# Two thirds of each feed-forward's way down as seven half-size products, behind the column tiles of the way up

## The chip, the cores and the metric

The kernel runs on one core of a Trainium2 chip. The metric is the device time of one execution in microseconds. Times before are from three runs; one further execution was profiled, and all views of the trace are of that one.

## The reference

A decoder trunk of two layers on 512 tokens of width 1024, all in float32. Layer 0 mixes tokens by dilated attention, layer 1 by a recurrent block (RG-LRU); each is followed by a feed-forward, and each of the four parts sits between two RMS norms:

```python
def conv_ffn(x, w_up, conv_w, conv_b, w_down):
    u = causal_dwconv(x @ w_up, conv_w, conv_b)
    g, v = u[..., :D_FF], u[..., D_FF:]
    return (jax.nn.gelu(g, approximate=True) * v) @ w_down

for layer in range(DEPTH):
    h = rms_norm(x, norm_mix_pre[layer])
    h = attention or rglru (h)
    x = x + rms_norm(h, norm_mix_post[layer])
    h = rms_norm(x, norm_ffn_pre[layer])
    h = conv_ffn(h, ffn_w_up[layer], ...)      # 1024 -> 2 x 3072 -> 1024
    x = x + rms_norm(h, norm_ffn_post[layer])
```

The change is in the two feed-forwards alone.

## The kernel before

**A matrix product.** Every float32 operand is split in two float32r parts, `hi` (a copy by ScalarE) and `lo` (the remainder, by VectorE), and three matmuls stand for one: hi x hi, hi x lo, lo x hi (`PASSES`, `mm3`). A weight goes from DRAM into a `raw` tile of 1 MB (two buffers), from there in two pieces ("units" of 128 x 1024) into `whi` and `wlo` (`pump`, `low_parts`), of which eight are held. The list `plan`, written at the end of the program, sets which weights are loaded and in which order they are split; `splits` keeps that order. `tick` is called after each piece of TensorE work: it lets waiting side work go on and splits one or two more units. Every engine takes its instructions in the order in which the program issues them.

**The way up.** The 6144 columns of `w_up` are cut in column tiles of 128 features by 512 tokens (`feat`: 8 x 3 matmuls of 512 columns, bank `ps`). A step of `j` has two gate tiles and two value tiles; each gets a convolution over tokens (one ScalarE step, two VectorE steps), the gate tile a gelu, the value tile a multiply with its gate tile. The results are `gv[0]` to `gv[23]`, 24 tiles of 128 x 512 that are the operand of the way down.

**Sevenths.** `PAIRS` lists which two steps go together. In a pair marked True the gate columns of both steps, a product of 512 tokens x 1024 x 512 columns, are computed by seven half-size products instead of eight (Strassen's scheme as arranged by Winograd), each 24 matmuls of 256 columns into a bank `vq`. The token sums `T` that they need are made once a layer. Sums of weights are not computed by an engine: they come up in the tile `sum`, into which POOL's queue adds one corner after the other with accumulating DMAs (`add_up`; kinds `first`, `sum`, `mix`), each allowed once the units of the one before have been split (`after`, `finished`).

**The way down.** `rows_proj` and `rows_run` multiply `gv` with the 3072 rows of `w_down`, 12 chunks of 256 rows: for each of four token tiles two banks `acc` of 512 columns, 24 x 3 matmuls each. When a token tile is complete, `norms` runs as side work: `postnorm` (L511 to L518), `prenorm`, and the transposes `tr` into the `hT` of the next layer. The last feed-forward has no `prenorm`, and its `postnorm` sends out the result.

In attention the values of two head groups are also made by seven products, of 512 columns each (`product`, L965); that function is moved by the change, so that the feed-forward can call it too.

**Memory.** `x` slots: eight tiles of 128 x 1024 that hold the residual, token sums or raw weights in turn. `gen` tiles: 29 of 128 x 512, for `gv` and all else. The `sum` tile and the norms' gains share one buffer.

Of the kernel before, what the change touches and what calls it, by code (L numbers as in the profile page):

```python
# [11 lines left out]
F32 = mybir.dt.float32  # L12
# [80 lines left out]
def kernel(  # L93
# [82 lines left out]
    raws, units, late = {}, {}, []  # L176
    sides, first_tiles = [], []

    total = {"open": True, "tile": None, "next": 0}
    finished, after, todo = set(), {}, {}  # L180

    def add(kind, kd, cols, srcs, behind=None, own=True):
# [99 lines left out]
    def add_up(i):  # L282

        kind, kd, cols, srcs = plan[i]
        if total["tile"] is None:
            total["tile"] = cp.tile([P, 512 // cols, 4, cols], F32, tag="gain", name=nm("sum"))
        tile_, at = total["tile"], 0
        part = tile_[:, int(kind[-1] == "1")]
        for src, m in srcs:
            dst = part[:, :, at : at + m]  # L290
            if kind[:5] == "first":
                nc.sync.dma_start(dst, src)
            else:
                nc.gpsimd.dma_start(dst, src, accum_op=ALU.add)
            at += m
        raws[i] = tile_ if kind == "mix" else part
        total["next"] += 1
# [219 lines left out]
            if final:  # L517
                nc.sync.dma_start(out[0, t * P : (t + 1) * P, i * 512 : (i + 1) * 512], xh[i])  # L518

    def norms(t, banks, post_g, pre_g, hT, spill):  # L520
        state["hold"] = t >= 2
        postnorm(t, banks, post_g, hT is None)
        if spill:
            nc.sync.dma_start(spill[t], xs_sb[t])
        if hT is not None:
            yield from prenorm(t, hT, pre_g, 3 if t == 3 else 4)
        if t == 3:
            state["hold"] = False
            total["open"] = True
# [14 lines left out]
    def token_sums(hT):  # L544
# [37 lines left out]

        return (lambda name: lambda a: made[name][a]), make

    def feat_tiles(n, hT, sink, halves=False, between=None, at=None):

        if halves:
            ids = [chunk() for _ in range(n)]
            W = {}
            banks = [psum() for _ in range(2 * n)]  # L590
            for hf in range(2):
                for j in range(2 * n):
                    if not hf:
                        W[j] = take(ids[j // 2], j % 2)
                    feat(W[j], hT, banks[j], hf * 256, hf * 256 + 256)
                    if hf:
                        done()
                        sink(j, banks[j])
                    tick()
            return  # L600
        for c in range(n):
            i = chunk() if at is None else at
            for m in range(2):
                ps = psum()
                feat(take(i, m), hT, ps, 0, S)
                done()
                sink(2 * c + m, ps)
                tick()
                if between:
                    between()  # L610

    def rows_proj(nchunks, act, order, post, pre, spill=None):
# [12 lines left out]
        def run():  # L625
            return rows_run(nchunks, A, prep, seq, order, post, pre, spill)

        return prep, run

    def rows_run(nchunks, A, prep, seq, order, post, pre, spill):  # L630
        total.update(open=False, tile=None)
        post_g, pre_g = gains(*[g for g in (post, pre) if g is not None])
        hT = new_hT() if pre is not None else None
        W, banks = {}, {}
        left = {}
# [3 lines left out]
        for tiles, chunks in order:  # L639
            for c in chunks:  # L640
                if c not in W:
                    i = chunk()
                    W[c] = (i, 0), (i, 1)
                last = len(tiles) == 1
                if last:
                    prep(seq.index(2 * c) + 4)
                    loop = [[(tiles[0], i, kk) for i in range(2) for kk in range(2)]]
                else:
                    loop = [[(t, i, kk) for t in tiles for i in range(2)] for kk in range(2)]
                for n, part in enumerate(loop):  # L650
                    prep(seq.index(2 * c + n) + 3)
                    for t, i, kk in part:
                        k = 2 * c + kk
                        if t not in banks:
                            banks[t] = [psum("acc"), psum("acc")]
                            left[t] = [2 * nchunks, 2 * nchunks]
                        mm3(
                            banks[t][i],
                            [a[:, t * P : (t + 1) * P] for a in A[k]],
                            [v[:, 0, i * 512 : (i + 1) * 512] for v in take(*W[c][kk])],  # L660
                            left[t][i] == 2 * nchunks,
                            left[t][i] == 1,
                        )
                        left[t][i] -= 1
                        uses[k] -= 1
                        if not uses[k]:
                            done()
                    for t in tiles:
                        if left[t] == [0, 0]:
                            side(norms(t, banks[t], post_g, pre_g, hT, spill))  # L670
                    tick()
        state["rows"] = False
        return hT
# [69 lines left out]
    def ffn(layer, hT, post, pre, spill):  # L743
# [15 lines left out]
        def gated(b, ps, k):  # L759
# [5 lines left out]
            else:  # L765
                gv[k] = u

        total_of, make = token_sums(hT)

        def sevenths(j, n):  # L770
# [55 lines left out]

            side(ends())

        order = [([0, 1, 2, 3], range(9)), ([0], range(9, 12)), ([1], range(9, 12))]
        order += [([2, 3], [9]), ([2], [10, 11]), ([3], [10, 11])]  # L830
        prep, run = rows_proj(12, act_split(gv), order, post, pre)
        for js, wide in PAIRS:
            n = state["next"]
            steps = sevenths(js[0], n) if wide else None
            at = iter(WIDE_STEPS if wide else (0,) * 16)

            def between():
                for _ in range(next(at)):
                    next(steps, None)
                    tick()  # L840

            for j in js:
                if j == 11:
# [7 lines left out]
                feat_tiles(1 if wide else 2, hT, sink, j == 0, between, (n + 3 + 3 * (j - js[0])) if wide else None)  # L851
            if wide:
                state["next"] += 9
        for t in range(4):
            xs_sb[t] = load_x(t, src=spill[t])
        return run()

    def attention(hT, post, pre, spill):
# [96 lines left out]
                    vs.append(o)  # L955
                tick()

        def product(banks, act):
            i = chunk()
            for j in range(2):  # L960
                W = take(i, j)
                for u in range(2):
                    for k in range(2):
                        for n, (a, b) in enumerate(PASSES):
                            mm(  # L965
                                banks[u],
                                act(a)[:, 2 * j + k, u * P : (u + 1) * P],
                                W[b][:, k, :],
                                start=(j, k, n) == (0, 0, 0),
                                stop=(j, k, n) == (1, 1, 2),  # L970
                            )
                done()

        def value_steps(p0):

            vds = [dp.tile([S, 512], F32, name=f"vrows{p0 + i}") for i in range(2)]
            vrows.update({p0: vds[0], p0 + 1: vds[1]})
            def two():
                return [psum("vq") for _ in range(2)]
# [6 lines left out]
            def each(dst, a, b, op):  # L986
                for u in range(2):
                    nc.vector.tensor_tensor(dst[u], a[u], b[u], op=op)

            def steps():  # L990
                q = two()
# [7 lines left out]
                each(o, c, q, ALU.add)  # L999
                out(0, 0, o)  # L1000
                yield
                chunk()
                q = two()
                y = [gen(s="y") for _ in range(2)]
                product(q, total_of(3))
# [14 lines left out]
                each(o, y, q, ALU.subtract)  # L1020
                out(1, 0, o)
                yield
                chunk()
                q = two()
                product(q, total_of(1))
                each(y, y, q, ALU.add)
# [379 lines left out]
    def value_part(*at):  # L1406
        if at in VALUE_STEPS:
            for q in next(parts):
                n = w_quarter(*q, behind=chain[-1])
                if q[0] == "sum":  # L1410
                    chain.append((n, 1))

    for hp in range(4):
        if hp % 2 == 0:
            w_value(qkv, (2 * D + hp * 256, 512))
# [9 lines left out]
    for layer in range(2):  # L1425
        if layer:
# [6 lines left out]
            for c in range(4):  # L1433
                w_rows(lru_w_out[0], c * 256, "pair")
        w_up, ends = ffn_w_up[layer], {}
        for js, wide in PAIRS:
            if not wide:
                for j in js:
                    w_cols(w_up, j * 256)
                    w_cols(w_up, D_FF + j * 256)  # L1440
# [80 lines left out]
```

## Time and profile before

| | |
|---|---|
| median of 3 runs | 1470.57 us (1470.45 to 1471.04) |
| profiled execution | 1470.15 us, of which the span is 1468.4 |
| granted TensorE clock | 0.996 of full speed |
| TensorE busy | 1455.4 us, 99% of the span |
| VectorE, ScalarE, GpSimd busy | 64%, 45%, 5% |
| feed-forward of layer 0 | way up 523.4 to 781.5 us, way down to 913.8 us |
| feed-forward of layer 1 | way up 1072.8 to 1330.9 us, way down to 1461.5 us |
| after the last matmul | 6.9 us |

The stages are read from the chain that ended last, which runs through TensorE nearly everywhere. "PE" is TensorE's matmuls, "PEld" its weight loads, "DVE" VectorE, "ACT" ScalarE, "POOL" GpSimd, which here only issues DMAs, "SP" the queue that issues the other DMAs. A row of the trace's groups reads: line, engine, operation, out<-in, shapes, count, busy us, mean ns of one, idle time just before and who ended it. A wait of one engine for another costs time only where TensorE waits in turn.

### The profile page before, as it was taken

The page shows a single profiled execution, that of the slowest core. Times are in us where ns is not written, and L with a number is a line of the kernel's source. Part 1 is how long each engine was busy: PE and PEld are TensorE (multiplying, and loading weights), DVE is VectorE, ACT ScalarE, POOL GpSimd, SP SyncE. Part 2 cuts the span into 40 slices and gives each one's busy share as a digit, 9 for nine tenths or more (in the row PEclk, how much of TensorE's full clock was granted, in tenths as well). Part 3 has the DMA queues.
Part 4 walks back from the last instruction along what each step waited for, and adds up shares of the span by engine and source line. Part 5 has one row for each costly group of instructions (what it writes and reads, how often), then busy time and mean ns, then how long its engine had stood idle before and what let it go on. Part 6 is the DMA issues. An engine that isn't in the chain of part 4 may idle for free.

```text
span 1468.4 us, 19295 instructions
## 1 busy us (share of the span) xinstructions
PE 1455.4 (99%) x7625; PEld 1249.3 (85%) x7625; DVE 933.5 (64%) x1627; ACT 658.1 (45%) x1098; POOL 78.2 (5%) x91
## 2 busy tenths in 40 slices
PE   8999999999999999999999999999999999999998
PEld 6788888888888898999988888988798899988886
DVE  5366444464445679888775337778779888775333
ACT  5344333253445454454544334479454454544221
POOL 0111100110000001001100000000001000000000
PEclk9999999999999999999999999999999999999999
DMA  5666457664336154576645203231344576555101
GB/s 197 213 197 159 126 152 207 151 180 156 110 109 217 58 166 117 163 186 145 172 168 197 95 29 115 87 115 44 129 150 109 159 186 154 148 181 191 58 1 58
DMA packets 152650, 203.86 MB, mean 139 GB/s; under 512 B 5895, under 2 KB 129295, under 8 KB 152560
## 3 DMA queue, kind: packets, MB, share of 16 engines
q1 hardware_dynamic: 128064, 170.64, 34.5%
q0 software_dynamic: 24496, 31.99, 11.6%
q8 instruction: 60, 0.98, 0.3%
q14 instruction: 30, 0.25, 0.1%
HBM read 189.98 MB, written 17.34 MB: 141 GB/s over the span
## 4 chain that ended last, share of the span: by engine, by line
PE 94%; DVE 2%; ACT 2%; DMA 1%; issue 0%; SPq 0%; DVEq 0%
PE ps L416 46%; PE acc L416 22%; PE vq L416 11%; PE vq L965 5%; PE v L939 3%; PE gate L416 1%; PE tr L465 1%; PE S L1126 1%; PE O L1098 1%; PE S L1063 1%; PE O L1194 1%; DMA raw<-in_attn_w_qkv_dram 1%; DVE wlo L249 1%; PE PT L1085 0%; PE PT L1175 0%
## 5 line engine op out<-in xcount | busy, mean ns | idle before, releaser
L416 PE MATMUL ps<-hT,whi 128*128 128x512 f32 (+1 forms) x2240 | 645.4, 373 | 0.0
L416 PEld LDWEIGHTS ps<-hT,whi 128*128 128x128 f32 x2240 | 404.7, 189 | 70.9 <-issue 1.3
L416 PE MATMUL ps<-hT,wlo 128*128 128x512 f32 (+1 forms) x1120 | 415.9, 371 | 0.0
L249 DVE TENSOR_TENSOR wlo<-raw,whi 128x1024 fp32r<-128x1024 f32 x244 | 295.2, 1219 | 137.0 <-ACT whi L240 136.4
L240 ACT ACTIVATE whi<-raw 128x1024 fp32r<-128x1024 f32 x244 | 253.1, 1053 | 183.5 <-PE acc L416 124.4
L416 PEld LDWEIGHTS ps<-hT,wlo 128*128 128x128 f32 x1120 | 211.1, 188 | 36.8
L416 PE MATMUL acc<-whi,ahi 128*128 128x512 f32 x512 | 200.6, 392 | 1.3 <-ACT ahi L171 1.3
L416 PE MATMUL acc<-whi,alo 128*128 128x512 f32 x512 | 199.6, 390 | 0.0
L416 PE MATMUL acc<-wlo,ahi 128*128 128x512 f32 x512 | 199.3, 389 | 0.0
L752 DVE SCALAR_TENSOR_TENSOR u<-ps,cols,u 128x511 f32<-128x511 f32 (+1 forms) x128 | 95.7, 748 | 49.6 <-ACT u L748 47.3
L416 PEld LDWEIGHTS acc<-whi,ahi 128*128 128x128 f32 x512 | 96.2, 188 | 21.2 <-ACT ahi L171 1.7
L416 PEld LDWEIGHTS acc<-whi,alo 128*128 128x128 f32 x512 | 96.1, 188 | 20.5 <-DVE alo L172 0.4
L416 PEld LDWEIGHTS acc<-wlo,ahi 128*128 128x128 f32 x512 | 96.2, 188 | 19.5
L416 PE MATMUL vq<-T,whi 128*128 128x256 f32 x512 | 93.4, 283 | 0.0
L416 PEld LDWEIGHTS vq<-T,whi 128*128 128x128 f32 x512 | 81.4, 192 | 1.9
L748 ACT ACTIVATE u<-ps,cols 128x512 f32<-128x512 f32 x64 | 49.2, 769 | 53.0 <-PE ps L416 52.9
L416 PE MATMUL vq<-T,wlo 128*128 128x256 f32 x256 | 72.5, 283 | 0.0
L762 ACT ACTIVATE u<-u 128x512 f32<-128x512 f32 x48 | 30.3, 632 | 90.2 <-DVE u L752 90.2
L416 PE MATMUL vq<-hT,whi 128*128 128x256 f32 x384 | 69.7, 283 | 0.0
L240 ACT ACTIVATE whi<-sum 128x1024 fp32r<-128x1024 f32 x40 | 41.7, 1049 | 47.2 <-DMA sum<-in_attn_w_qkv_dram 47.2
L416 PEld LDWEIGHTS vq<-hT,whi 128*128 128x128 f32 x384 | 60.4, 192 | 0.6
L249 DVE TENSOR_TENSOR wlo<-sum,whi 128x1024 fp32r<-128x1024 f32 x40 | 48.5, 1219 | 15.6 <-ACT whi L240 15.6
(211 smaller groups left out, 1671.6 us busy)
## 6 DMA issues: line engine op xcount, KB each, us to landing
raw<-in_ffn_w_up_dram SPq DMA_DIRECT2D x40, 1024.0 KB
raw<-in_attn_w_qkv_dram SPq DMA_DIRECT2D x26, 1024.0 KB
raw<-in_ffn_w_down_dram SPq DMA_DIRECT2D x12, 1024.0 KB
raw<-in_ffn_w_down_dram SPq DMA_DIRECT2D x24, 512.0 KB
raw<-in_attn_w_qkv_dram SPq DMA_DIRECT2D x16, 512.0 KB
sum<-in_attn_w_qkv_dram POOLq DMA_DIRECT2D x16, 512.0 KB, 7.7
sum<-in_ffn_w_up_dram SPq DMA_DIRECT2D x16, 512.0 KB
sum<-in_ffn_w_up_dram POOLq DMA_DIRECT2D x16, 512.0 KB, 7.8
```

Source lines behind the costliest of these rows:

```text
L240: nc.scalar.activation(hi, raw, AF.Copy)
L249: nc.vector.tensor_tensor(lo, raw, hi.bitcast(F32), op=ALU.subtract)
L416: mm(dst, l[a], r[b], start=start and n == 0, stop=stop and n == 2)
L465: nc.tensor.transpose(ps[:, k * P : (k + 1) * P], xs[i][:, k * P : (k + 1) * P], ident)
L748: nc.scalar.activation(u, ps, AF.Identity, scale=cc[:, j : j + 1], bias=cc[:, 48 + j : 49 + j])
L752: nc.vector.scalar_tensor_tensor(u[:, d:], ps[:, : S - d], wc, u[:, d:], op0=ALU.mult, op1=ALU.add)
L762: nc.scalar.activation(u, u, AF.Gelu_apprx_tanh)
L939: mm(banks[t], hT[a][:, k, t * P : (t + 1) * P], W[b][:, k % 2, :], start=(k, a, b) == (0, 0, 0), stop=(k, a, b) == (KD - 1, 1, 0),)
L965: mm(banks[u], act(a)[:, 2 * j + k, u * P : (u + 1) * P], W[b][:, k, :], start=(j, k, n) == (0, 0, 0), stop=(j, k, n) == (1, 1, 2),)
L1063: mm(Sp[a // 2][:, o + lo : o + 256], q[hh][:, a * P : (a + 1) * P], k[hh][:, k0 : (a + 1) * P], start=True, stop=True)
L1098: mm(po[:, a * P : (a + 1) * P], pts[a, j], vtile(v, a - 1 + j, h % 4), start=j == js[0], stop=j == 1)
L1126: mm(ps[:, c], q[hh][:, c], k[hh][:, c], start=True, stop=True)
```

## The change

`w_down` is taken in three thirds of 1024 rows. For two of them (`DOWN_UNITS = 2`), the product of 512 tokens x 1024 x 1024 columns is made by seven half-size products of 256 tokens x 512 x 512 columns, each 24 matmuls of 512 columns into two banks `vq`. They run while the way up is still going: `DOWN_AT` names the column tiles, counted from step 6 on (24 tiles), behind which one product stands. The operands `A` are sums of pieces of `gv`, made by VectorE and split as usual (`operands`); two are made ahead, and behind each product the one for the product after the next is begun. The weights are quarters of 512 rows x 512 columns; for four of the seven products they are sums and come up in the `sum` tile by accumulating DMAs of 1 MB (`down_quarters`). The first unit's results (eight tiles of 128 x 512) are written to DRAM; the second unit's stay in `gen` tiles, and at the start of the rows POOL's queue adds the first unit's to them (`gather`, eight DMAs of 256 KB). The last third of `w_down`, four chunks, goes through `rows_run` as before, in the order `SHORT_ORDER`, in which the recurrent layer's way out (also four chunks) already runs; its token tiles get the gathered tiles added at the start of `norms` (`extra`). Two of the four pairs by sevenths, steps 6 to 9, become plain.

```diff
-PAIRS = [([0, 1], False), ([2, 3], True), ([4, 5], True), ([6, 7], True), ([8, 9], True), ([10, 11], False)]
+PAIRS = [([0, 1], False), ([2, 3], True), ([4, 5], True), ([6, 7], False), ([8, 9], False), ([10, 11], False)]
+DOWN_FROM = 6
+DOWN_UNITS = 2
+DOWN_AT = (3, 5, 6, 7, 8, 9, 12, 13, 15, 16, 17, 18, 19, 22)
...
-    def norms(t, banks, post_g, pre_g, hT, spill):
+    def norms(t, banks, post_g, pre_g, hT, spill, extra):
         state["hold"] = t >= 2
+        if extra:
+            more = extra(t)
+            each(more, banks, more, ALU.add)
+            banks = more
         postnorm(t, banks, post_g, hT is None)
...
+            def step(combine):
+                op = ready.pop(0)
+                q = two()
+                product(q, lambda a: op[a])
+                begin_operand(ops)
+                write()
+                combine(q)
+                end_operand()
...
+        def gather():
+            for t in range(4):
+                for p in range(2):
+                    for d in downs:
+                        nc.gpsimd.dma_start(parts[t, p], d[place(t, p)], accum_op=ALU.add)
...
-        order = [([0, 1, 2, 3], range(9)), ([0], range(9, 12)), ([1], range(9, 12))]
-        order += [([2, 3], [9]), ([2], [10, 11]), ([3], [10, 11])]
-        prep, run = rows_proj(12, act_split(gv), order, post, pre)
+        first = 8 * DOWN_UNITS
+        act = act_split(gv)
+        prep, run = rows_proj(12 - first // 2, lambda k: act(first + k), SHORT_ORDER, post, pre, extra=extra, begin=gather)
...
             def between():
-                for _ in range(next(at)):
+                for _ in range(next(at, 0)):
                     next(steps, None)
                     tick()
+                if j >= DOWN_FROM:
+                    f = at_feat[0]
+                    if f < 2 or f in DOWN_AT:
+                        next(units)
+                    if f in DOWN_AT:
+                        if f == DOWN_AT[-2]:
+                            state["slots"] += 2
+                        tick()
+                    at_feat[0] += 1
...
+            q("value", 0, 0)
+            yield
+            q("first", 0, 0, ends["sum"])
+            one = q("sum", 0, 1)
+            yield
+            q("value", 1, 0)
+            yield
+            more = q("sum", 1, 1, (one, 1))
+            yield
+            q("value", 1, 1)
+            yield
+            all_ = q("sum", 1, 0, (more, 1))
+            yield
+            q("first", 0, 1, (all_, 1))
+            ends["sum"] = (q("sum", 1, 1), 1)
+            yield
...
-        for c in range(12):
+        for c in range(4 * DOWN_UNITS, 12):
             w_rows(ffn_w_down[layer], c * 256, "pair" if c % 2 else "rows")
```

How this moves instructions is seen at three places. VectorE in layer 0, before: the steps of two plain column tiles, each with its weight split behind it (`u` a tile of the way up, `ps` its bank).

```order
L752 SCALAR_TENSOR_TENSOR u_6788<-ps_6763,cols_1135,u_6788 128x511
L752 SCALAR_TENSOR_TENSOR u_6788<-ps_6763,cols_1135,u_6788 128x510
L764 TENSOR_TENSOR u_6710<-u_6710,u_6788 128x512
L249 TENSOR_TENSOR wlo_6756<-raw_6591,whi_6755 128x1024
L752 SCALAR_TENSOR_TENSOR u_6822<-ps_6797,cols_1135,u_6822 128x511
L752 SCALAR_TENSOR_TENSOR u_6822<-ps_6797,cols_1135,u_6822 128x510
```

VectorE in layer 0, now: behind the first unit's second product (`vq_6027`, `vq_6028`), the operand of its fourth (`A_6053` the high part, `A_6054` the low one), both weight units of the fourth product out of `sum`, and then the next column tile.

```order
L616 TENSOR_TENSOR y_5901<-c_5899,vq_6027 128x512
L616 TENSOR_TENSOR y_5902<-c_5900,vq_6028 128x512
L890 TENSOR_TENSOR A_6054<-A_5763,A_6053 128x1024
L252 TENSOR_TENSOR wlo_6022<-sum_5655,whi_6021 128x1024
L252 TENSOR_TENSOR wlo_6064<-sum_5655,whi_6063 128x1024
L787 SCALAR_TENSOR_TENSOR u_6097<-ps_6072,cols_1135,u_6097 128x511
L787 SCALAR_TENSOR_TENSOR u_6097<-ps_6072,cols_1135,u_6097 128x510
L799 TENSOR_TENSOR u_5974<-u_5974,u_6097 128x512
```

Combines, operands and two splits have moved in between column tiles, and the tile's steps stand behind them. ScalarE in layer 0, before, in the last plain pair: a weight split never comes from `sum`.

```order
L240 ACTIVATE whi_6715<-raw_6514 128x1024
L748 ACTIVATE u_6744<-ps_6719,cols_1139 128x512
L762 ACTIVATE u_6744<-u_6744 128x512
L748 ACTIVATE u_6749<-w_6400,cols_1139 128x512
L762 ACTIVATE u_6749<-u_6749 128x512
L240 ACTIVATE whi_6755<-raw_6591 128x1024
```

ScalarE in layer 0, now, ahead of the first unit's last product: `whi_6320` is the first half of that product's weights, and `u_6349` the first step of the column tile ahead of the sixth product.

```order
L243 ACTIVATE whi_6272<-raw_6152 128x1024
L884 ACTIVATE A_6302<-A_5763 128x1024
L243 ACTIVATE whi_6314<-raw_6188 128x1024
L243 ACTIVATE whi_6320<-sum_5655 128x1024
L783 ACTIVATE u_6349<-ps_6324,cols_1139 128x512
L797 ACTIVATE u_6349<-u_6349 128x512
```

The column tile's step and gelu now stand behind a split that needs a finished accumulation. VectorE at the end of the program, before: the last token tile's norm begins with its two banks `acc`.

```order
L511 TENSOR_TENSOR post_12461<-acc_11660,gain_11632 128x512
L427 TENSOR_SCALAR s_12464<-s_12463 128x1
L511 TENSOR_TENSOR post_12462<-acc_11661,gain_11632 128x512
L431 SCALAR_TENSOR_TENSOR s_12465<-s_12463,s_12464 128x1
L432 RECIPROCAL s_12466<-s_12466 128x1
```

VectorE at the end of the program, now:

```order
L616 TENSOR_TENSOR c_11330<-acc_12183,c_11330 128x512
L616 TENSOR_TENSOR y_11332<-acc_12184,y_11332 128x512
L515 TENSOR_TENSOR post_12341<-c_11330,gain_12024 128x512
L431 TENSOR_SCALAR s_12344<-s_12343 128x1
L515 TENSOR_TENSOR post_12342<-y_11332,gain_12024 128x512
L435 SCALAR_TENSOR_TENSOR s_12345<-s_12343,s_12344 128x1
```

Two adds of a bank to a gathered tile stand ahead of each token tile's norm.

More of the change, by code (lines that the diff above doesn't have):

```diff
@@ L583, in token_sums, with product, two, each @@
         return (lambda name: lambda a: made[name][a]), make
+    def product(banks, act):
+        i = chunk()
+        while plan[i][0] == "first":
+            i = chunk()
+        for j in range(2):
+            W = take(i, j)
+            for u in range(2):
+                for k in range(2):
+                    for n, (a, b) in enumerate(PASSES):
+                        mm(
+                            banks[u],
+                            act(a)[:, 2 * j + k, u * P : (u + 1) * P],
+                            W[b][:, k, :],
+                            start=(j, k, n) == (0, 0, 0),
+                            stop=(j, k, n) == (1, 1, 2),
+                        )
+            done()
+    def two(s="vq"):
+        return [psum(s) for _ in range(2)]
+    def each(dst, a, b, op):
+        for u in range(2):
+            nc.vector.tensor_tensor(dst[u], a[u], b[u], op=op)
     def feat_tiles(n, hT, sink, halves=False, between=None, at=None):
@@ L1001, in steps @@
                 yield
-                chunk()
                 q = two()
```

154 lines of the change are left out of this document (124 added, 30 removed).

## The prediction

> **What bounds the kernel now.** I read the page's busy times and its chain first, then the waits of TensorE, then the chain by stretches of time, and last the busy times of the other engines in the feed-forward's stretches.
>
> ```profile
> span 1468.4 us, 19295 instructions
> PE 1455.4 (99%) x7625; PEld 1249.3 (85%) x7625; DVE 933.5 (64%) x1627; ACT 658.1 (45%) x1098; POOL 78.2 (5%) x91
> PE 94%; DVE 2%; ACT 2%; DMA 1%; issue 0%; SPq 0%; DVEq 0%
> PE tr L465 <- DVE xs L501: 2.0, 2, 1.8
> PE acc L416 <- ACT ahi L171: 1.3, 1, 1.3
> ```
>
> The last two rows are waits of TensorE (total, times, longest): the first is from the kernel's start, the second from the recurrent layer's way out. There are three more, at the start or in attention and none over 1.5 us; no wait lies in a feed-forward. So the feed-forwards cost what their matmuls cost, and a matmul less is worth its time as long as nothing new makes TensorE wait. The price of a matmul comes from unbroken pieces of the chain (start, length, what, count):
>
> ```profile
> 256.07 10.88 PE vq L965 x48
> 709.75 8.63 PE vq L416 x72
> 737.94 43.55 PE ps L416 x192
> 1330.90 130.57 PE acc L416 x576
> ```
>
> On 512 columns, 43.55/192, 130.57/576 and 10.88/48 all give 0.2267 us; the third is attention's products, the very loop that the change now also uses. On 256 columns, 8.63/72 gives 0.1199 us, 13 ns more than half. I call 24 matmuls of 512 columns a group (5.44 us): one column tile of the way up is a group, one new product is a group.
>
> **The sum on TensorE.** Removed per layer: the way down, 12 chunks x 2 x 4 token tiles x 2 halves x 3 passes = 576 matmuls, keeps 4 chunks (192) and gets 14 products (336): 48 fewer, 96 in two layers, 96 x 0.2267 = 21.8 us. Added: a pair done by sevenths takes 7 x 24 = 168 matmuls of 256 columns, 168 x 0.1199 = 20.1 us; plain it takes 96 of 512 columns, 21.8 us. That is 1.63 us for each of four pairs, 6.5 us. Net -15.2 us. The count of the built program agrees: 384 matmuls fewer (-672 +384 -96).
>
> The Trainium skill (TensorE: Matmul & The Clock Gate, Back-to-back issue gap) gives columns/2.4 + 2.5 ns when warm, 215.8 and 109.2 ns; this would make the plain pairs 2.4 us dearer each and the sum -11.2 us. The rows above differ from it by 10 ns on both sizes, and they are this kernel's, so the measured prices stand.
>
> **What it does to the engines that TensorE waits for.** Prices:
>
> ```profile
> L249 DVE TENSOR_TENSOR wlo<-raw,whi 128x1024 fp32r<-128x1024 f32 x244 | 295.2, 1219 | 137.0 <-ACT whi L240 136.4
> L240 ACT ACTIVATE whi<-raw 128x1024 fp32r<-128x1024 f32 x244 | 253.1, 1053 | 183.5 <-PE acc L416 124.4 <-DMA raw<-in_attn_w_qkv_dram 25.0 <-DMA raw<-in_ffn_w_up_dram 16.9
> L752 DVE SCALAR_TENSOR_TENSOR u<-ps,cols,u 128x511 f32<-128x511 f32 x64 | 47.8, 747 | 47.3 <-ACT u L748 47.3
> L748 ACT ACTIVATE u<-ps,cols 128x512 f32<-128x512 f32 x64 | 49.2, 769 | 53.0 <-PE ps L416 52.9
> L762 ACT ACTIVATE u<-u 128x512 f32<-128x512 f32 x48 | 30.3, 632 | 90.2 <-DVE u L752 90.2
> L764 DVE TENSOR_TENSOR u<-u,u 128x512 f32<-128x512 f32 x48 | 33.2, 692 | 24.8 <-ACT u L762 24.3
> L793 DVE TENSOR_TENSOR w<-y,vq 128x256 f32<-128x256 f32 x32 | 11.9, 414 | 0.0
> L511 DVE TENSOR_TENSOR post<-acc,gain 128x512 f32<-128x512 f32 x32 | 21.8, 686 | 42.3 <-ACT junk L423 42.3
> ```
>
> VectorE, per column tile: one weight split 1.22, two convolution steps 1.49, every second tile a multiply 0.69: 3.06 us. Per product: two splits 2.44; the operand, on average (3 x 4 x 0.414 + 4 x (4 x 0.414 + 1.22)) / 7 = 2.35; and eight pairs of 512-wide combines per seven products, 16 x 0.69 / 7 = 1.58: 6.4 us. Where tile and product alternate, 9.4 us of VectorE stand beside 10.9 us of TensorE (87%). Stretches in which that was already so (columns: length, PE, PEld, DVE, ACT, POOL, clock, DMA share, GB/s):
>
> ```profile
> 574.00:616.00 42.00, 42.00 (x266) 38.17 (x265) 36.78 (x51) 18.59 (x24) 3.91 (x3) 1.00 0.62 158
> 737.94:781.49 43.55, 43.55 (x194) 36.05 (x193) 31.25 (x42) 22.27 (x30) 0.00 (x0) 1.00 0.45 164
> 830.00:880.00 50.00, 50.00 (x222) 41.39 (x222) 17.04 (x19) 15.31 (x20) 0.00 (x0) 1.00 0.14 45
> ```
>
> The first, a pair by sevenths, has VectorE at 36.78/42.00 = 88% and TensorE without a gap; the third is the way down, where VectorE is 66% idle and the work of the products used to hide easily. By the order, an operand begun behind product p is used in product p+2, three groups (16.3 us) after p ends; its low part stands behind p's combines (at most 2.8 us), itself 1.2, so VectorE may fall 12 us behind before TensorE notices. ScalarE has 1.05 + 0.77 + 0.32 a tile and about 4 a product, 6 of 10.9 us. I take no stall here, 0 to 3 us for the range.
>
> Weights of products 2, 4, 6 and 7 are added up by accumulating DMAs of 1 MB into the one `sum` tile, each after the last reader of the one before. The trace has only 512 KB ones; first their page row (median landing), then that of the first feed-forward (min, median, max):
>
> ```profile
> sum<-in_ffn_w_up_dram POOLq DMA_DIRECT2D x16, 512.0 KB, 7.8
> DMA to landing us min/median/max: 6.0/7.8/9.7
> ```
>
> 1 MB lies between 6.0 (if all is fixed cost) and 2 x 9.7 = 19.4 us; I take 2 x 7.8 = 15.6, since most of it should be bytes. Tightest is product 7 of a layer's first unit: the last reader of product 6's weights stands in VectorE's queue behind product 4's combines (2.8), an operand's low part (1.7) and two splits (2.4), done 6.9 us after product 4 ends. Then a plain 1 MB load (6.4 us at the 164 GB/s of the row above, queued behind writes), the accumulate, a high and a low part (2.3). Product 7 starts seven groups, 38.1 us, after product 4: 22.5 us are left for an accumulate of at most 19.4. Queued behind that wait on ScalarE stands the first step of the tile ahead of product 6: it starts some 10 us late, and one bank is held longer. TensorE has product 6 and three tiles with their weights ready meanwhile, four groups or 21.8 us. Taken: 0; range 0 to 4.
>
> **The way down's shorter rest and its ends.** Its 192 matmuls last 43.5 us, and the first token tile is complete 84 matmuls (19 us) in, where it used to be after 468 (106 us). Gains, the eight gathers (256 KB each, landing at most the 9.7 us above) and the reloaded x must be there by then. Gains and the first gathers follow the last read of `sum`, some 20 us ahead of the rows, so they have about 25 us to spare. x is queued on SP behind a load that waits for a split about 4 us into the rows: 512 KB at 164 GB/s take 3.2 us, so it lands about 10 us in. The nearest edge is on VectorE: product 14's combines, four splits, the last tile's steps and then the first `alo`, 7.3 us into the rows by the durations above, wanted by the 39th matmul at 8.6 us. Taken 0; range 0 to 2 in each layer.
>
> Each token tile now first adds two banks to the gathered tiles, 2 x 0.69 us on VectorE ahead of its norm. That shows at two places. The last rows of layer 0 (chain, then VectorE's own):
>
> ```profile
> 913.83 5.75 PE ps L416 x48
> 923.33 0.87 PE tr L465 x8
> 916.18 0.68 DVE L511 TENSOR_TENSOR post<-acc,gain 128x512 f32<-128x512 f32 x1
> 921.64 1.05 DVE L457 TENSOR_SCALAR xs<-xs,s,s 128x512 f32<-128x512 f32 x2
> ```
>
> Token tile 3's chain begins when tile 2's has ended (916.18) and is ready at 922.7 for transposes at 923.33: 0.6 us of slack. The adds lengthen both tiles' chains by 1.3 us each, since VectorE sets their pace: 2.7 - 0.6 = 2.1 us late; the first transpose needs only the first half of `xs`, 0.5 us earlier, but the second needs the rest. I take 2.0 us (1.5 to 2.7). At the very end:
>
> ```profile
> 1460.86 0.69 DVE L511 TENSOR_TENSOR post<-acc,gain 128x512 f32<-128x512 f32 x1 [1.16 <-ACT junk L423]
> 1462.22 0.69 DVE L511 TENSOR_TENSOR post<-acc,gain 128x512 f32<-128x512 f32 x1 [0.61 <-ACT junk L423]
> 1463.72 1.41 DVE L516 SCALAR_TENSOR_TENSOR x<-post,s,x 128x512 f32<-128x512 f32 x2
> ```
>
> The first bank is complete 6 matmuls (1.36 us) ahead of the second, which hides one add; the second add precedes the last square, which ends 0.7 us later. Taken +0.7 (0.7 to 1.4).
>
> Sum: the profiled execution took 1470.15 us; -15.2 + 2.0 + 0.7 = -12.5 gives 1457.6. The median of the runs shown, 1470.57, is 0.4 above the profiled one, so 1458.1.
>
> **Rivals.** (A, the forecast) all of this stays hidden but the two ends: 1458.1, between 1455.4 (-15.2, nothing else) and 1461. Chance 0.66.
>
> (B) The accumulates come late. It decides from 22.5 us each: beyond the row's largest doubled, but the DMA share in such stretches is 0.62. Product 7 of unit one and product 2 of unit two, twice each, 2 us late: +8, 1466. Chance 0.10.
>
> (C) Slower: VectorE becomes the bound where tile and product alternate, because its combines wait for the product's end with everything else queued behind. Ten such couples a layer in two runs of five; it decides when a couple loses over 12/5 = 2.4 us more than the 1.5 us of idle time it has. At 3.5 us a couple: 20 x 3.5 - 4 x 12 = +22, about 1480. Against it stands the 88% stretch without a gap. Chance 0.06.
>
> (D) The short rest of the way down starts or ends late (x, `alo`, first norm): 3 to 8 us, mostly in layer 0, where transposes follow: 1461 to 1466. For it speaks the 1.3 us of slack; chance 0.14.
>
> (E) The smaller sum of -11.2, if 256 columns in these four pairs were cheaper than the row: 1462.1. The pairs in question are half of the row's own; chance 0.02. This is the gap formula named above; the trace does not bear it out.
>
> The remaining 0.02 I leave to something slower that I do not see. That the change does nothing is excluded by the count.
>
> **Numbers.** Within 0.2% is 2.9 us, about what a measurement of this kernel can tell from no change. Faster: A, D, E and most of B, 0.89; same: the rest of B and the edge of C, 0.04; slower: C and the unseen, 0.07. The range runs from A's lower bound to past B's 1466: 1455 to 1467.
>
> **What would show it.** In the changed profile: about 7241 matmuls; groups of 24 at 5.44 us for `vq` out of `A`; no wait of TensorE between the pairs and the rows; a wait of about 2 us at the `tr` of layer 0's last token tile; a tail of 7.6 instead of 6.9 us. Wrong if TensorE waits for `whi` or `wlo` out of `sum` (B), for `A` (C), or for `ahi`, `alo` or an earlier `tr` (D).

## The result and the profile after

| | median us | range | runs | ratio to the kernel before (95%) |
|---|---|---|---|---|
| before | 1470.8 | 1470.45 to 1472.8 | 4 | |
| after | 1457.45 | 1457.16 to 1457.99 | 4 | 0.9907 (0.989 to 0.9924) |

The change takes 13.3 us off (the table has a fourth run of the kernel before, 1472.8, so its median is 1470.8). The forecast was 1458.1, and its likeliest case (A, everything hidden but the two ends) is what happened. The experiments below show that one margin behind that forecast was reckoned wrongly, and that a second error covered it up.

Head of the page of the changed kernel, with the shares of its chain:

```profile
span 1456.2 us, 18714 instructions
PE 1438.8 (99%) x7241; PEld 1221.8 (84%) x7241; DVE 1005.2 (69%) x1763; ACT 681.0 (47%) x1142; POOL 97.5 (7%) x111
PE 88%; DVE 5%; ACT 4%; DMA 1%; issue 1%; SPq 0%; DVEq 0%; ACTq 0%
```

Three rows of TensorE's waits (who waited, for whom, total us, times, longest):

```profile
PE tr L469 <- DVE xs L505: 3.9, 2, 3.7
PE acc L420 <- ACT ahi L174: 2.0, 1, 2.0
PE tr L469 <- DVE xs L461: 1.4, 1, 1.4
```

TensorE still sets the time, with 384 matmuls fewer. The first row lies ahead of the first feed-forward and was 2.0 us before; the second is the recurrent layer's, 1.3 us before. The third is new and is the one forecast at layer 0's last token tile. No wait holds up the matmuls of a feed-forward. The prices are those of before; the chain (start, length, what, count):

```profile
584.32 8.63 PE vq L420 x72
850.38 5.44 PE vq L602 x24
1405.25 43.53 PE acc L420 x192
```

A product (`vq` L602) is 24 matmuls in 5.44 us and the shorter way down 192 in 43.53. Each feed-forward, from its first `ps` to its last `acc`, went from 390.4 to 382.6 us in layer 0 and from 388.6 to 380.8 in layer 1: 7.8 each, where 7.6 was forecast. With that the two profiled spans add up: 15.6 us less in the feed-forwards, 0.6 more ahead of the first, 2.4 more between them, 0.5 more after the last matmul, 12.2 in all. Stretches of the first one (length, PE, PEld, DVE, ACT, POOL, clock, DMA share, GB/s), all three with products:

```profile
698.00:752.50 54.50, 54.50 (x242) 45.15 (x241) 44.20 (x65) 26.74 (x36) 2.58 (x2) 1.00 0.64 175
752.50:807.00 54.50, 54.50 (x242) 45.13 (x241) 42.64 (x58) 25.46 (x33) 3.85 (x3) 1.00 0.76 193
807.00:861.50 54.50, 54.50 (x242) 45.16 (x241) 39.86 (x53) 23.47 (x32) 9.52 (x11) 1.00 0.74 215
```

TensorE fills all of them; VectorE is at 73 to 81% where the products run, below the 87% of a couple that the forecast worked with, because not every tile has a product behind it.

### The profile page after: what moved, and what is told of

Same layout as the page of the kernel before. It is cut to its first block, busy times and chain, and to the rows that moved or that the text cites. A ratio compares the mean times of both kernels' runs of the same rounds, so it can differ in the third digit from the quotient of the medians.

```text
span 1456.2 us, 18714 instructions
## 1 busy us (share of the span) xinstructions
PE 1438.8 (99%) x7241; PEld 1221.8 (84%) x7241; DVE 1005.2 (69%) x1763; ACT 681.0 (47%) x1142; POOL 97.5 (7%) x111
## 4 chain that ended last, share of the span: by engine, by line
PE 88%; DVE 5%; ACT 4%; DMA 1%; issue 1%; SPq 0%; DVEq 0%; ACTq 0%
PE ps L420 49%; PE vq L602 16%; PE acc L420 10%; PE vq L420 6%; PE v L1124 3%; DVE xb L1461 1%; DVE wlo L252 1%; PE S L1286 1%; PE tr L469 1%; PE O L1258 1%; PE S L1223 1%; DMA raw<-in_attn_w_qkv_dram 1%; PE O L1354 1%; DVE th L1513 1%; ACT whi L243 0%
## 5 line engine op out<-in xcount | busy, mean ns | idle before, releaser
L420 PE MATMUL ps<-hT,whi 128*128 128x512 f32 (+1 forms) x2496 | 723.8, 374 | 0.0
L420 PEld LDWEIGHTS ps<-hT,whi 128*128 128x128 f32 x2496 | 453.6, 188 | 82.0 <-issue 1.3
L420 PE MATMUL ps<-hT,wlo 128*128 128x512 f32 (+1 forms) x1248 | 465.4, 373 | 0.0
L602 PE MATMUL vq<-whi,A 128*128 128x512 f32 x448 | 142.4, 389 | 0.0
L420 PE MATMUL acc<-whi,ahi 128*128 128x512 f32 x256 | 101.0, 394 | 2.0 <-ACT ahi L174 2.0
L420 PE MATMUL acc<-whi,alo 128*128 128x512 f32 x256 | 99.9, 390 | 0.0
L420 PE MATMUL acc<-wlo,ahi 128*128 128x512 f32 x256 | 99.7, 389 | 0.0
L602 PEld LDWEIGHTS vq<-whi,A 128*128 128x128 f32 x448 | 84.1, 188 | 17.4
L602 PE MATMUL vq<-wlo,A 128*128 128x512 f32 x224 | 87.1, 389 | 0.0
L420 PEld LDWEIGHTS acc<-whi,ahi 128*128 128x128 f32 x256 | 48.1, 188 | 11.9 <-ACT ahi L174 2.4
L602 PEld LDWEIGHTS vq<-wlo,A 128*128 128x128 f32 x224 | 42.0, 188 | 8.7
```

The source lines that it names most:

```text
L420: mm(dst, l[a], r[b], start=start and n == 0, stop=stop and n == 2)
L602: mm(banks[u], act(a)[:, 2 * j + k, u * P : (u + 1) * P], W[b][:, k, :], start=(j, k, n) == (0, 0, 0), stop=(j, k, n) == (1, 1, 2),)
```

## The experiments

Every time below is a median in us, beside runs of the kernel before on the same chip (1470.2 to 1470.7). "Above after" is against 1457.45.

### The pairs alone, and the adds alone

The kernel before, with its pairs of steps 6 to 9 made plain and nothing else changed:

```diff
-([6, 7], True), ([8, 9], True)
+([6, 7], False), ([8, 9], False)
```

> The kernel before with steps 6 to 9 plain and nothing else: no products, the old way down. Theory (TensorE is the only bound, the price of a pair is the difference of its matmuls): the trace's pair by sevenths lasts 42.0 us and a plain pair 43.55, so four plain pairs add 4 x 1.55 = 6.2 us, about 1477. Rival (the pairs by sevenths cost more elsewhere, in sums of weights and VectorE's load, so that plain pairs are free): 1471.

Measured: 1476.02 (ratio 1.004, 1.0027 to 1.0054), 5.75 above before. The plain pairs cost what the theory said, a little less: a pair by sevenths, 168 x 0.1199 + 96 x 0.2267 = 41.9 us by the two prices, takes 42.0 us on the chain of the changed kernel (584.32 to 626.32), and a plain pair, 192 matmuls, 43.53. That is 1.5 us a pair where 1.63 was taken. With two pairs a layer, it accounts for the 0.2 us a layer by which the feed-forwards gained more than forecast.

The changed kernel without the two VectorE additions per token tile:

```diff
-more = extra(t); each(more, banks, more, ALU.add); banks = more
+extra(t)
```

> The changed kernel without the two adds ahead of each token tile's norm; the norm takes the banks alone, so two thirds of the way down are missing from the output. Theory: the wait of TensorE at the last transposes of layer 0 (1.4 us) and 0.5 us of the tail go, 1455.5 us. Rival (the wait comes from the shorter rest of the way down, with gains, x or the first token tiles late): the wait stays, 1457.

Measured: 1455.07 (0.9898, 0.9883 to 0.9914). The additions at the two ends cost 2.4 us (2.7 forecast), and without them the 1.4 us wait at `tr` is gone from the list. So the 13.3 us come from -21.8 of matmuls (count times price, no run of its own), +5.7 of plain pairs and +2.4 of additions (both by the runs): -13.7, which leaves 0.4 that no run assigns.

### How much VectorE can carry

Six, and then three, further additions of 128x256 behind every product:

```diff
 combine(q)
+for _ in range(6):   # 3 in the second kernel
+    nc.vector.tensor_tensor(spare, still, still, op=ALU.add)
 end_operand()
```

> The changed kernel with six more VectorE additions of 128 x 256 behind each product (6 x 0.415 = 2.5 us, 28 products; their result is not used). Theory (VectorE may fall about 12 us behind before TensorE notices): a couple of tile and product then needs 11.9 us of VectorE beside 10.9 of TensorE, 1 us lost a couple, 5 in a run of five: hidden, 1457.5 to 1459. Rival (VectorE is at its limit there): at least 1 us for each of 20 couples, 1477 or more.

Measured: 1481.3 (1.0076, 1.0063 to 1.009), 23.9 above after. The theory that VectorE has that room fell, but the loss is not in the couples either. TensorE's waits in this kernel:

```profile
PE acc L420 <- DVE alo L175: 13.6, 2, 6.8
PE acc L420 <- DVE wlo L252: 3.3, 2, 1.7
```

The stretches about the first feed-forward's first rows (columns as above):

```profile
861.50:879.00 17.50, 9.03 (x38) 6.72 (x36) 16.60 (x24) 10.15 (x14) 3.56 (x4) 0.84 0.97 243
879.00:925.00 46.00, 46.00 (x230) 39.28 (x231) 34.79 (x86) 17.55 (x43) 0.00 (x0) 0.95 0.45 152
```

The timeline of TensorE behind that gap (start, length, what):

```profile
882.15 0.63 PE L420 MATMUL acc<-whi,ahi 128*128 128x512 f32 x1
882.58 0.63 PE L420 MATMUL acc<-wlo,ahi 128*128 128x512 f32 x1
```

Both waits are at the start of the rows, one of each in each layer: VectorE's queue, in order, has a backlog of the products' stage in front of the rows' first `alo`, which starts at 878.26 here and at 867.70 in the changed kernel. The first stretch shows it: in 17.50 us VectorE is busy 16.60 and TensorE 9.03. After that gap the matmuls stand 0.43 us apart (starts of the two rows) from 879.0 to 883.4, at a granted clock of 0.84 and 0.95 in the two stretches: the gap is paid once more in slow matmuls, some ten here, 2 us. The Trainium skill (TensorE: Matmul & The Clock Gate, Part 1) says that after an idle window of about 3.4 us the array runs at half rate and gives 426.7 ns for 512 columns; this trace agrees on the rate: from 879.59 to 883.43 nine matmuls start 0.427 us apart. A single wait of that length is not needed, as the last experiment shows.

The backlog is not VectorE's alone. In the first feed-forward the chain of this execution leaves TensorE at 665.6 and comes back at 879.00. Besides VectorE's work it passes five transfers into `sum`, 35 us together, such as these two (a plain load and its accumulate):

```profile
735.00 5.10 DMA sum<-in_ffn_w_down_dram
740.75 8.23 DMA sum<-in_ffn_w_down_dram
```

A late VectorE frees the tile late, and the split that then waits for the next sum holds the queues in turn. What VectorE can hide is therefore a margin that it shares with the sums. The additions were not run without the accumulates, so the two parts are not told apart.

> The changed kernel with three more VectorE additions of 128x256 (0.42 us each) behind every product: 14 x 1.26 = 17.6 us of VectorE a layer, half of the run with six. Theory now: the products' stage hides some 23 us a layer and only what goes beyond that shows, where the rows begin: nothing shows, 1457 to 1460. Rival: the time grows with each us of VectorE work, as 24/70 of it: +12, 1469.

Measured: 1457.28 (0.9911, 0.9896 to 0.9926), as the theory said. 17.6 us of VectorE work a layer are hidden whole; of 35 us, 23 are. The same 35 us put behind one unit's products alone:

```diff
-for _ in range(6):
+for _ in range(12 if unit == 0 else 0):   # unit == 1 in the second kernel
```

> The 84 additions a layer of the run with six behind every product, now twelve behind each of the first unit's seven products and none behind the second's: 35 us of VectorE a layer as there. Theory: what is late in unit one is made up in unit two's idle time (about 26 us of VectorE) before the rows begin; TensorE may wait once or twice in unit one, 0 to 4 us a layer: 1458 to 1466. Rival (only the sum of VectorE's work in the stage counts): 1481 as with six behind each.

> The same 84 additions, twelve behind each of the second unit's seven products. Theory: all of it stands ahead of the rows' first low parts, with only unit two's idle time (some 26 us, at most half of it usable) to hide it: 10 to 20 us a layer visible beyond the six-run's share, 1485 to 1500. Rival (only the sum counts): 1481.

Measured: 1492.48 (1.0147, 1.0129 to 1.0164) and 1494.94 (1.0164, 1.0149 to 1.0179). The waits of the first kernel, then of the second:

```profile
PE vq L602 <- DVE wlo L252: 16.7, 8, 3.5
PE ps L420 <- DVE wlo L252: 9.0, 4, 2.6
```

```profile
PE acc L420 <- DVE alo L175: 13.0, 2, 6.5
PE acc L420 <- DVE wlo L252: 9.0, 3, 4.4
```

My expectation for unit two came true; the one for unit one was wrong: a backlog is not made up later once TensorE has waited for it, and with 5 us more per couple it waits for a low part at about every second product. The rival (only the sum counts) is wrong too: both kernels take longer than 1481. Of 35 us a layer, 17.5 are hidden when all stand in unit one, 16.3 in unit two, and 23 when they are spread. The two units' margins do not add up, or the spread 35 would be hidden whole; that what is late in unit one passes on to unit two would explain it, but is not shown. What shows also includes the slow matmuls behind the waits. The place of the wait is where the work stands: inside unit one, or at the rows behind unit two.

### A version with one pair less made plain

The pair of steps 6 and 7 by sevenths again, so that the 14 products stand behind 14 of the last 16 tiles instead of 14 of 24 (the first two operands are then made during the pair before; shortened here):

```diff
-([6, 7], False)   DOWN_FROM = 6   DOWN_AT = (3, 5, 6, 7, 8, 9, 12, 13, 15, 16, 17, 18, 19, 22)
+([6, 7], True)    DOWN_FROM = 8   DOWN_AT = (0, 1, 2, 3, 4, 5, 6, 8, 9, 10, 11, 12, 13, 14)
```

> The changed kernel with steps 6 and 7 again by sevenths, so that only one pair is plain, and the 14 products behind 14 of the last 16 column tiles. Theory: 2 x 1.55 = 3.1 us less on TensorE, 1454.4, if VectorE (87% busy in couples of tile and product, now seven in a row) and the chain of sums keep up. Rival (the chain of sums has only one spare tile left, VectorE none): new waits of TensorE for weights out of sum of 2 to 4 us a layer eat the gain, 1456 to 1462.

Measured: 1475.37 (1.0032, 1.002 to 1.0043), 21 above its matmul count, outside both expectations. Its profiled execution, 1470.75, is the lowest of its six; the chain has two places at the end of the first feed-forward where TensorE is not on it. The first:

```profile
749.29 2.28 DVE wlo L252 x2
751.59 5.47 DMA sum<-in_ffn_w_down_dram
757.71 8.15 DMA sum<-in_ffn_w_down_dram
765.88 1.06 ACT whi L243
770.33 1.88 PE vq L602 x7
```

A split of one sum ends, a plain load into `sum` runs, an accumulate follows, then the splits, then TensorE: the sums are made in one tile, one after the other, and here that chain was late. While ScalarE waits for it, everything behind it in its queue waits too. At the rows there is a second stop behind a 15.74 us load of `w_down` weights. I first held VectorE's backlog at the rows for the cause, and took 10 us of VectorE's work a layer to GpSimd:

```diff
-nc.vector.tensor_tensor(run[:, k], ...)
+nc.gpsimd.tensor_tensor(run[:, k], ...)
```

> The run with three pairs by sevenths (1475.4), with the operands' 24 sums a layer of 128x256 taken from VectorE and done on GpSimd: VectorE loses 24 x 0.42 = 10 us a layer. Theory: VectorE's lag where the rows begin was that kernel's loss, so most of it goes: 1456 to 1464. Rival: GpSimd takes over 2 us for such an addition, four in a row make the operand late for its product (two groups, 10.9 us, behind), 1475 or more.

Measured: 1482.31 (1.0084, 1.0058 to 1.0109), worse, as the rival said (the profiled execution, 1488.61, is the slowest of its four). Four such sums take 3.3 to 3.8 us on GpSimd (start to end) against 1.4 on VectorE, operands come late (`vq` waits for `A` 9.5 us in all), and VectorE itself loses time beside it. Its groups in the first feed-forward's products, in the changed kernel (the version with three pairs has the same means within 1 ns) and then in this one:

```profile
L787 DVE SCALAR_TENSOR_TENSOR u<-ps,cols,u 128x511 f32<-128x511 f32 (+1 forms) x46 | 34.4, 748 | 31.6 <-ACT u L783 30.7
L799 DVE TENSOR_TENSOR u<-u,u 128x512 f32<-128x512 f32 x15 | 10.4, 692 | 3.4 <-ACT u L797 3.0
L893 DVE TENSOR_TENSOR A<-u,A 128x256 fp32r<-128x256 f32 x24 | 8.5, 417 | 1.8 <-ACT A L887 1.8
```

```profile
L787 DVE SCALAR_TENSOR_TENSOR u<-ps,cols,u 128x511 f32<-128x511 f32 (+1 forms) x34 | 25.4, 747 | 5.8 <-ACT u L783 5.2
L799 DVE TENSOR_TENSOR u<-u,u 128x512 f32<-128x512 f32 x14 | 15.6, 1112 | 6.3 <-ACT u L797 6.1
L893 DVE TENSOR_TENSOR A<-u,A 128x256 fp32r<-128x256 f32 x24 | 13.9, 641 | 1.7 <-ACT A L887 1.7
```

The multiply of two SBUF tiles goes from 692 to 1112 ns in the mean, the operand's low part from 417 to 641; the convolution step, which reads one input from a PSUM bank, stays at 747. The means hide what happens: 12 of the 14 multiplies still take 0.69 us, and two wait until a run of GpSimd's four sums is over. One of them, GpSimd's row first:

```profile
733.06 3.33 POOL L880 TENSOR_TENSOR A<-A,u 128x256 f32<-128x256 f32 x4
733.32 3.63 DVE L799 TENSOR_TENSOR u<-u,u 128x512 f32<-128x512 f32 x1
```

The Trainium skill (SBUF — State Buffer, Who interferes with whom) says that a VectorE instruction with two SBUF inputs contends with a GpSimd instruction that reads SBUF, and one with a single SBUF input does not; these rows agree.

### What the accumulates can cost

Each 1 MB accumulate sent twice:

```diff
-nc.gpsimd.dma_start(dst, src, accum_op=ALU.add)
+for _ in range(2 if m == 512 else 1):
+    nc.gpsimd.dma_start(dst, src, accum_op=ALU.add)
```

> The changed kernel with each accumulating DMA of 1 MB sent twice, one behind the other (the sums then hold the added half twice, so the products' values are wrong; times only). Theory: these transfers land after 8.8 us where the prediction took 15.6, and the tightest, product 7 of unit one, had its splits 10.8 us ahead of need, so 8.8 us more is hidden there or nearly; product 2 of unit two may be some 5 us late in each layer: 1457 to 1468. Rival (the transfers cost what the prediction took, 15.6 us each, of 22.5 to be had): 9 us late at two products a layer, 1475 or more.

Measured: 1579.27 (1.0747, 1.073 to 1.0763), 122 above after: the theory fell, and though the rival's "1475 or more" takes it in, its working (9 us at two products a layer, 36 in all) does not. TensorE's two largest waits:

```profile
PE vq L603 <- ACT whi L243: 34.5, 6, 6.9
PE vq L603 <- DVE wlo L252: 28.8, 15, 3.3
```

A piece of its chain in the second feed-forward:

```profile
1324.02 8.33 DMA sum<-in_ffn_w_down_dram
1332.73 12.20 DMA sum<-in_ffn_w_down_dram
```

ScalarE's timeline in the first (in brackets its idle time before, and what ended it):

```profile
770.83 1.06 ACT L243 ACTIVATE whi<-sum 128x1024 fp32r<-128x1024 f32 x1 [20.37 <-DMA sum<-in_ffn_w_down_dram]
```

ScalarE is blocked for 20.37 us by one sum. A layer has eight accumulates; the added ones land after 9.1 us (median of the first feed-forward), 73 us a layer, and 61 a layer show. The lateness is handed on from sum to sum. GpSimd's issues of a layer's first and last accumulate, in the changed kernel and then here (the second of two):

```profile
661.56 1.28 POOL L298 DMA_DIRECT2D sum<-in_ffn_w_down_dram  x1 [35.76 <-DMA sum<-in_ffn_w_down_dram]
823.81 1.29 POOL L298 DMA_DIRECT2D sum<-in_ffn_w_down_dram  x1 [26.80 <-DVE A L880]
```

```profile
670.20 1.28 POOL L299 DMA_DIRECT2D sum<-in_ffn_w_down_dram  x1 [7.61 <-DMA sum<-in_ffn_w_down_dram]
885.03 1.28 POOL L299 DMA_DIRECT2D sum<-in_ffn_w_down_dram  x1 [8.60 <-DMA sum<-in_ffn_w_down_dram]
```

The eight (the second of each two) come 8.6, 14.0, 20.3, 31.6, 37.7, 49.3, 56.1 and 61.2 us later than in the changed kernel. By the program each load into `sum` waits for the splits of the sum before, so the single tile makes them one chain; ScalarE's queue, which is in order, ties it to the rest. Some 12 us of 73 are absorbed in a whole layer. The chain's own spare time may be larger: of the first feed-forward's 61 us TensorE waits for 40, and the rest is mostly matmuls at half rate behind the waits.

The opposite, with no 1 MB accumulate at all, in the changed kernel and in the version with three pairs by sevenths:

```diff
-else:
+elif m < 512:
     nc.gpsimd.dma_start(dst, src, accum_op=ALU.add)
```

> The changed kernel without the sixteen accumulating DMAs of 1 MB (the products that need a sum of two quarters get one quarter alone; times only). Theory: in the changed kernel they are hidden whole, so it stays at 1457.4, 1456.5 to 1458. Rival: some of them are on TensorE's path already and hidden from the list of waits: 1455 or less.

Measured: 1456.71 (0.9909, 0.9894 to 0.9924; 1456.09 to 1457.79): 0.7 less than after, with overlapping ranges. In the changed kernel the accumulates are hidden.

> The kernel with three pairs by sevenths (1475.4), again without the sixteen accumulating DMAs of 1 MB (same remark). Theory: its products follow each other every 10.9 us, and the chain load, accumulate, splits on the single `sum` tile was what it had no time for; without the accumulates most of the 21 us above the 1454.4 of its matmul count goes: 1455 to 1463. Rival (VectorE's backlog alone was its loss): the same work stands on VectorE, 1470 or more.

Measured: 1454.88 (0.9895, 0.9879 to 0.9912), against 1475.37 with them and 1454.4 by the matmul count. So the accumulates were that version's whole loss: no wait for a weight or for `ahi` and `alo` is left in its feed-forwards, at the rows neither, and VectorE's work, with the same instructions, did not cause it alone. Whether the stop at the rows came from the accumulates' bytes or from the order that they forced is not told apart. A second `sum` tile, which might lift this, was not run, so the tile is not told apart from ScalarE's in-order queue either; nothing here beats the changed kernel with its full work.

### The wait at the last transposes

```diff
-([2, 3], [1]), ([2], [2, 3]), ([3], [2, 3])
+([2], [1, 2, 3]), ([3], [1, 2, 3])          # layer 0 only
```

> The changed kernel; in layer 0's short way down token tiles 2 and 3 take their last three chunks one tile after the other (36 matmuls each), where chunk 1 was shared, so tile 2 is complete 36 instead of 24 matmuls (8.2 instead of 5.4 us) before the end. Theory: the wait of 1.4 us at the last tile's transposes was VectorE's, still on tile 2's norm, so it goes: 1456.0. Rival: the wait only moves, because six weight units stay in use longer and the next layer's first splits come late: 1457.5 to 1460.

Measured: 1464.74 (0.9965, 0.9952 to 0.9977), 7.3 above after. The wait for `xs` went, as the theory said, and the rival took its place, dearer than it had put it. Two of TensorE's new waits:

```profile
PE ps L423 <- DVE wlo L178: 1.8, 1, 1.8
PE ps L423 <- ACT whi L246: 1.7, 1, 1.7
```

The two stretches in question, in the changed kernel and then here:

```profile
905.00:915.00 10.00, 10.00 (x80) 9.73 (x80) 9.61 (x30) 4.05 (x13) 0.00 (x0) 1.00 0.56 180
915.00:935.00 20.00, 18.62 (x147) 17.89 (x147) 15.60 (x26) 11.20 (x17) 1.09 (x2) 1.00 0.31 106
```

```profile
905.00:915.00 10.00, 8.68 (x65) 7.89 (x64) 9.65 (x28) 5.52 (x16) 0.92 (x2) 1.00 0.01 2
915.00:935.00 20.00, 15.78 (x91) 15.13 (x92) 7.84 (x11) 6.11 (x8) 0.17 (x1) 0.74 0.60 190
```

With three chunks still in use nothing of the next layer is loaded (DMA share 0.01, 2 GB/s, where the changed kernel has 0.56 and 180); then its first tiles wait for weights, and the clock falls to 0.74 in the next 20 us, where it was 1.00. No wait here is longer than 1.8 us, yet after two of them, 1.11 and 1.78, matmuls of 256 columns start 0.21 us apart instead of 0.12: waits of less than 3.4 us cost slow matmuls too.

## Why the prediction was right, and which step was not

- **Matmul count and prices.** Right: 7241 matmuls, 5.44 us a product, 43.53 us for the short way down. A plain pair costs 1.5 us more, not 1.63, which makes the sum 0.4 us better.
- **The two ends.** Right in place, a little large: the wait at the last `tr` is 1.4 us (2.0 taken), the time after the last matmul went from 6.9 to 7.4 (7.6 forecast). That is 1.9 by the trace and 2.4 by the run without the additions; the difference is not accounted for.
- **VectorE in the couples (0 to 3 us).** The 0 held, but the argument pointed to the wrong place. "12 us behind before TensorE notices" counted an operand; what TensorE notices is a weight's low part inside unit one, or the first `alo` behind unit two. Between 16 and 23 us of added work a layer is hidden, depending on where it stands, and by the chain of the run with six additions the sums share that margin. Rival C's mechanism exists, but not at its point: six additions are 2.5 us a couple, 1 us beyond the idle time, which by its rule would show nothing, and 24 us showed.
- **The accumulates: the step that failed.** The transfers were forecast at 15.6 us each, with 22.5 to be had at the tightest place. The transfers into `sum` in the products' stage of the changed kernel:

```profile
DMA to landing us min/median/max: 8.4/8.8/10.6
```

  The splits of unit one's product 7 by the timelines of ScalarE and VectorE:

```profile
741.73 1.06 ACT L243 ACTIVATE whi<-sum 128x1024 fp32r<-128x1024 f32 x1 [9.56 <-DMA sum<-in_ffn_w_down_dram]
748.61 1.22 DVE L252 TENSOR_TENSOR wlo<-sum,whi 128x1024 fp32r<-128x1024 f32 x1
```

  And that product on the chain:

```profile
757.90 5.44 PE vq L602 x24
```

  They land after 8.8 us in the median: twice the bytes of the 512 KB ones (7.8; as many rows, half as long) cost 1 us more, so the step from 7.8 to 15.6 was wrong. The splits of product 7 end at 749.8; its second half, which needs them, begins 2.7 us after 757.90: 10.8 us of slack. So the margin at that one place was reckoned about right. What failed is that the working gave each accumulate a margin of its own. They share one tile, so when one is late the next is late too, and ScalarE's queue spreads it: some 12 us were absorbed for all eight of a layer, not 10.8 for each. At the 15.6 us that the prediction took, eight times 6.8 us more would be 54 us a layer, of which, as an estimate from the doubled run, some 42 would show: slower than before, not 1458. A price too high and a margin counted eight times cancelled, so that this term came out at 0 by luck. ScalarE blocked "some 10 us" (9.56) was right.
- **The rows' start (1.3 us of slack).** Right: the first `alo` run starts at 867.70, its first ends at about 868.3, for the 39th matmul, 8.6 us after 861.26. It is the edge at which the added VectorE work showed.

```profile
867.70 3.09 DVE L175 TENSOR_TENSOR alo<-u,ahi 128x512 fp32r<-128x512 f32 x5
```

- **Rivals.** D and E did not come; B stayed hidden in this kernel and is what decided its denser version, at 21 us where B was priced at 8 for this one.

## What to carry to other kernels

Work that is hidden behind TensorE has a margin per queue and per buffer, not per instruction: follow the buffer's reuse through all its users in turn and add their latenesses, above all where transfers of many microseconds go through one tile. Double the suspected transfer and remove it; the two runs show how much slack it has where the list of waits shows nothing. A denser schedule that saves matmuls (here 3 us) can cost seven times as much once such a chain has no slack.

## What the runs showed of the hardware

- An accumulating DMA of 1 MB into `sum` lands after 8.8 us, one of 512 KB (as many rows, half as long) after 7.8, both medians of the first feed-forward; twice the bytes add an eighth.
- While GpSimd adds SBUF tiles, a VectorE multiply with two SBUF inputs can be held until a whole run of four such sums is over (3.63 us instead of 0.69); the convolution steps with one input from a bank take what they did (747 ns).
- After a wait of 6.8 us TensorE's next ten matmuls stood about 0.43 us apart instead of 0.227; two waits of 1.1 and 1.8 us were also followed by matmuls at about half rate.
